# A hybrid backbone step on one core: gate prefix sums in blocks of 384 tokens, outer products two steps later

## The chip, the cores and the metric

The kernel runs on one core of one Trainium2 chip. The metric is the device time of one execution in microseconds; the lower the better. A comparison shows the median of several executions.

## What is computed

Two layers over 1152 tokens (128 context tokens and 1024 latent tokens) of width 1024. Each layer has a token mixer with three groups (attention, gated linear attention GLA, and a gated recurrence RG-LRU) that share one input projection and one output projection, and then an MLP with 4096 hidden units. The part that the change touches is GLA: for each direction, gates `g` are summed along each chunk of 64 tokens, and queries and keys are scaled by the exponentials of those sums.

```python
def gla_chunked(q, k, v, g, s0):                      # n chunks of 64 tokens, H = 4 heads of 64
    b = jnp.cumsum(g, axis=2)                         # the prefix sums, per chunk
    b_last = b[:, :, -1:]
    q_in, k_in, k_end = q * jnp.exp(b), k * jnp.exp(-b), k * jnp.exp(b_last - b)
    a_intra = jnp.where(causal, jnp.einsum('bnchd,bnshd->bnhcs', q_in, k_in), 0.0)
    o_intra = jnp.einsum('bnhcs,bnshv->bnchv', a_intra, v)
    delta = jnp.einsum('bnchd,bnchv->bnhdv', k_end, v)
    # s = exp(b_last) * s + delta, from chunk to chunk; s_before is the state ahead of a chunk
    o_inter = jnp.einsum('bnchd,bnhdv->bnchv', q_in, s_before)
    return o_intra + o_inter, s_final
# token_mixer: h @ w_in -> q k v gq gk gv gz gr lx lg; attention, gla_mixer (both directions),
# rglru_mixer (conv, two gates, scan in both directions); concat @ w_out
```

## The kernel before, and what sets its order

Activations lie with features on the partitions and tokens along the columns, in blocks of 384 tokens (`TB`; `NTB` is 3). Each projection of 128 output features is a `dense` of 24 matmuls for each block (eight slices of 128 input features, and for each the three products L156, L157, L158 of values split into a high and a low part). Its result stands in one of two PSUM banks `pd` and is evicted by VectorE (DVE) or ScalarE (ACT): gq by L491 on DVE, gr by L516 on ACT and L517 on DVE, lg by L524 to L530, k and q by L552, L553 on DVE. With two banks, the matmuls of a block can start when the block two before it is evicted.

Only TensorE's (PE's) order is written by hand; a scheduler at build time orders the other engines. The projections run in the order gv0, gk0, gz, gq0, gr0, gv1, gk1, gq1, lx0, gr1, lx1, lg0, lg1, k, v, q0 to q3. Between their matmuls everything else of the mixer is handed out in steps: `dense` calls `tick` after each half of a block (12 matmuls), and `tick` takes the next step of the first generator in a chain, up to its next `yield`. A projection has six such steps. The chain holds `gla_pair(0)` from gz on, then `gla_pair(1)`, then `lru_all` (the recurrence, for `t` = 0 and 1). A generator starts when the one ahead of it has ended. Ahead of q2 the chain is drained: whatever is left is issued at once.

`gla_pair(pair)` treats two heads (`hf` = 0, 1), both directions on the two halves of the partitions. Its steps: gate products (L592) and their logarithms (L600); `cum(hf)`, the subtract L605 (DVE for `hf` 0, GpSimd (POOL) for `hf` 1) and the prefix sums L606 (forward) and L607 (backward) as scans of all 1152 columns, with `smask` zero at the start of every chunk; six passes, one for each head and block, of `pre` (L647 and L650 on DVE, an exponential L649 on ACT), `trans` (L656 on PE, L658 on ACT) and `delta` (L667 on PE, L676, L678, L683 on ACT, L684 on POOL); `states` (scans L692); then, for each block, `intra` (L731 on PE; L733 and L737 on DVE, the sum of both directions' masked scores), `outer` (L745, L751), `headsum` (L762) and `gate` (L774). `lru_all` has the convolution L827, gate matmuls, products L868, L871, and for each direction the square root L884, a product L886 and the scan L890; then L898, L900 and the store of the result to `mixd`. The first output projection (L1218 to L1220, ahead of attention) reads `mixd` back (L1189), casts it (L1194) and splits it (L1195).

Of the kernel before, what the change touches and what calls it, by code (L numbers as in the profile page):

```python
# [10 lines left out]
ALU = mybir.AluOpType  # L11
# [10 lines left out]
NTB = T // TB  # L22
# [17 lines left out]
def blk(t, tb):  # L40
    return t[:, tb * TB:(tb + 1) * TB]
# [8 lines left out]
class Net:  # L50
# [390 lines left out]
    def mixer(self, l):  # L441
        nc, I, O, C = self.nc, self.I, self.O, self.C
# [130 lines left out]
        def gla_pair(pair, hook):  # L573
# [10 lines left out]
            mns = []  # L584
# [16 lines left out]

            def cum(hf):
                Bt = G2[:, hf]
                eng = nc.gpsimd if hf else nc.vector
                eng.tensor_tensor(Bt, Bt, mns[hf], ALU.subtract)  # L605
                nc.vector.tensor_tensor_scan(Bt[0:64], smask[0:64], Bt[0:64], 0.0, ALU.mult, ALU.add)  # L606
                nc.vector.tensor_tensor_scan(Bt[64:128, ::-1], smask[64:128], Bt[64:128, ::-1], 0.0, ALU.mult, ALU.add)  # L607
                qd, kd = B(), B()
                for d in range(2):
                    nc.sync.dma_start(kd[64 * d:64 * d + 64], self.gkd[pair][64 * hf:64 * hf + 64])  # L610
                H.append((Bt, qd, kd))

            def load_qd(hf):
                for d in range(2):
                    nc.sync.dma_start(H[hf][1][64 * d:64 * d + 64], self.gqd[pair][64 * hf:64 * hf + 64])

            cum(0)
            for _ in range(3):
                yield
            steps = [(hf, tb) for hf in range(2) for tb in range(NTB)]  # L620
            st = {}

# [19 lines left out]
            def pre(hf, tb):  # L642
                if tb == 0:
                    start(hf)
                Bt, qd, kd = H[hf]
                e = self.tn()
                nc.vector.tensor_tensor(e.rearrange("p (c s) -> p c s", s=64), blk(Bt, tb).rearrange("p (c s) -> p c s", s=64),  # L647
                                        st[hf][4][:, 6 * tb:6 * tb + 6].unsqueeze(2).to_broadcast([128, 6, 64]), ALU.subtract)
                nc.scalar.activation(e, e, AF.Exp, scale=1.0 / 16)  # L649
                nc.vector.tensor_tensor(e, blk(kd, tb), e, ALU.mult)  # L650
                return e
# [49 lines left out]
                nc.gpsimd.tensor_copy(Sc[f, 0:2], dlv[f, 0:2])  # L701

            e = pre(*steps[0])
            for _ in range(3):
                yield
            cum(1)
            prev = None
            for n in range(len(steps) + 1):
                cur = None
# [72 lines left out]
            for hf in range(2):  # L782
                As[hf] = intra(0, hf)
                yield
            yield
            for tb in range(NTB):
                oT, sq = outer(tb, As)
# [120 lines left out]
        def lru_fin():  # L908
# [5 lines left out]

        self.lru_fin = lru_fin
        order = [("gv0", ev_nat(self.gvd[0]), None), ("gk0", ev_st(self.gkd[0]), None), ("gz", ev_gz, lambda: self.add(gla_pair(0, lambda: None))),
                 ("gq0", ev_st(self.gqd[0], 0.125, "v"), None), ("gr0", ev_r(self.grd[0]), None),
                 ("gv1", ev_nat(self.gvd[1]), None), ("gk1", ev_st(self.gkd[1]), lambda: self.add(gla_pair(1, lambda: next(lin[0], None)))),
                 ("gq1", ev_st(self.gqd[1], 0.125, "v"), None), ("lx0", ev_st(self.lxd[0]), None),
                 ("gr1", ev_r(self.grd[1]), None), ("lx1", ev_st(self.lxd[1]), lambda: self.add(lru_all())),  # L920
# [19 lines left out]
        smask = gp.tile([128, T], mybir.dt.bfloat16, name="smask")  # L940
# [600 lines left out]
```

## Time and profile before

| | |
|---|---|
| median of 3 runs | 2908.7 us (2908.16 to 2912.33) |
| the profiled execution | 2908.05 us, its span 2906.2 us |
| busy share of the span | PE 95%, DVE 50%, ACT 39%, POOL 28% |
| mean granted PE clock | 0.977 of full |
| the two mixers | about 98 to 433 us and 1515 to 1856 us of the span |

PE works nearly all the time, so what counts is when it does not: the times at which it waits, and for whom, and the stretches in which its granted clock is 0.5. The DVE, ACT and POOL rows matter only where PE waits for them. A matmul of 384 columns is shown with 0.34 us but the next starts 0.17 to 0.18 us after it, since they overlap.

### The profile page before, as it was taken

Reading aid. Unit: us, or ns where it says so; the run is one execution under the profiler, and the core shown is the slowest. Engines: PE = TensorE matmul, PEld = TensorE weight load, DVE = VectorE, ACT = ScalarE, POOL = GpSimd, SP = SyncE. Lnnn points to the kernel's source line nnn. Section 1 sums busy time; section 2 is a strip of 40 time slices with the busy share of each in tenths; the row PEclk is TensorE's granted clock in tenths of the full one; section 3 lists DMA queues with packets and bytes.
Section 4 is the critical chain, followed back from the end, with each engine's and each line's share of the span. In section 5 each row is a group of like instructions: output and inputs, shape, how many; then the busy total and the mean of one; then the engine's idle time right before and its main releaser. Section 6 shows DMA issues by size and latency. Waiting matters only on the chain. (4 is left out here: it accounts for less than half of the span.)

```text
span 2906.2 us, 41527 instructions
## 1 busy us (share of the span) xinstructions
PE 2748.9 (95%) x16067; PEld 2625.6 (90%) x16067; DVE 1455.2 (50%) x2577; ACT 1119.6 (39%) x2046; POOL 802.5 (28%) x848
## 2 busy tenths in 40 slices
PE   5898899999999999999988989899899999999998
PEld 4887897889999999999987879878899999999998
DVE  7645677795332333233475547778832333233235
ACT  4645447763112212211356436477612112211223
POOL 4234447742001001100223244576311001100112
PEclk7999999999999999999999999999999999999999
DMA  7545358421321111111343643662211111111113
GB/s 263 137 124 158 99 157 253 128 80 51 95 88 38 43 44 44 44 37 44 111 120 86 175 127 102 217 210 69 73 37 44 44 44 39 42 44 44 44 37 131
DMA packets 279301, 273.64 MB, mean 94 GB/s; under 512 B 30032, under 2 KB 259008, under 8 KB 279104
## 3 DMA queue, kind: packets, MB, share of 16 engines
q1 hardware_dynamic: 278888, 270.92, 30.5%
q8 instruction: 127, 2.08, 0.3%
q14 instruction: 70, 0.57, 0.1%
q10 hardware_dynamic: 216, 0.06, 0.0%
HBM read 227.02 MB, written 43.91 MB: 93 GB/s over the span
## 5 line engine op out<-in xcount | busy, mean ns | idle before, releaser
L119 ACT CAST wh<-wr 128x1024 fp32r<-128x1024 f32 x228 | 239.0, 1048 | 923.5 <-PE pg L157 822.4
L157 PE MATMUL pg<-hl,wh 128*128 128x384 f32 x1584 | 538.3, 340 | 3.2 <-DVE hl L358 1.7
L156 PE MATMUL pg<-hh,wh 128*128 128x384 f32 x1584 | 538.4, 340 | 1.8 <-ACT hh L351 1.8
L158 PE MATMUL pg<-hh,wl 128*128 128x384 f32 x1584 | 537.3, 339 | 0.0
L1261 POOL TENSOR_TENSOR te<-te 128x384 f32<-128x384 f32 x192 | 165.9, 864 | 1332.9 <-ACT uh L1260 1332.7
L158 PE MATMUL pg<-uh,wl 128*128 128x384 f32 x1536 | 513.5, 334 | 1.7 <-DVE wl L120 1.7
L156 PE MATMUL pg<-uh,wh 128*128 128x384 f32 x1536 | 514.4, 335 | 0.6 <-ACT wh L119 0.6
L157 PE MATMUL pg<-ul,wh 128*128 128x384 f32 x1536 | 513.2, 334 | 0.0
L1283 DVE SCALAR_TENSOR_TENSOR x<-pg,mod,x 128x384 f32<-128x384 f32 (+2 forms) x512 | 254.2, 515 | 395.7 <-PE pg L158 395.4
L120 DVE TENSOR_TENSOR wl<-wr,wh 128x1024 fp32r<-128x1024 f32 x196 | 245.1, 1251 | 213.0 <-ACT wh L119 213.0
L1262 DVE TENSOR_TENSOR ul<-te,uh 128x384 fp32r<-128x384 f32 x192 | 107.1, 558 | 453.4 <-POOL te L1261 453.4
L156 PE MATMUL pd<-hh,wh 128*128 128x384 f32 x816 | 295.3, 362 | 22.2 <-DVE te L491 11.1
L157 PEld LDWEIGHTS pg<-hl,wh 128*128 128x128 f32 x1584 | 299.1, 189 | 5.6 <-DVE hl L358 3.0
L156 PEld LDWEIGHTS pg<-hh,wh 128*128 128x128 f32 x1584 | 299.3, 189 | 5.4 <-issue 3.4
L158 PEld LDWEIGHTS pg<-hh,wl 128*128 128x128 f32 x1584 | 299.3, 189 | 0.0
L156 PEld LDWEIGHTS pg<-uh,wh 128*128 128x128 f32 x1536 | 288.3, 188 | 4.3 <-DVE x L1283 1.7
L158 PEld LDWEIGHTS pg<-uh,wl 128*128 128x128 f32 x1536 | 288.3, 188 | 2.3 <-DVE wl L120 2.2
L157 PEld LDWEIGHTS pg<-ul,wh 128*128 128x128 f32 x1536 | 288.4, 188 | 0.0
L157 PE MATMUL pd<-hl,wh 128*128 128x384 f32 x816 | 285.1, 349 | 3.4 <-DVE hl L392 3.4
L158 PE MATMUL pd<-hh,wl 128*128 128x384 f32 x816 | 284.0, 348 | 0.0
L1259 ACT ACTIVATE te<-pg 128x384 f32<-128x384 f32 x192 | 93.8, 489 | 360.2 <-PE pg L158 360.2
L156 PEld LDWEIGHTS pd<-hh,wh 128*128 128x128 f32 x816 | 161.3, 198 | 30.7 <-DVE te L491 12.1
(279 smaller groups left out, 4341.7 us busy)
## 6 DMA issues: line engine op xcount, KB each, us to landing
wr<-in_w_mlp_dram SPq DMA_DIRECT2D x144, 512.0 KB, 4.0
wm<-in_w_mod_dram SPq DMA_DIRECT2D x96, 512.0 KB, 4.9
wr<-in_w_out_dram SPq DMA_DIRECT2D x48, 512.0 KB, 4.9
wr<-in_w_in_dram SPq DMA_DIRECT2D x36, 512.0 KB, 5.2
xd<-x SPq DMA_DIRECT2D x48, 192.0 KB, 3.6
x<-xd SPq DMA_DIRECT2D x48, 192.0 KB, 3.9
raw<-mixd SPq DMA_DIRECT2D x40, 192.0 KB, 2.9
B<-gkd SPq DMA_DIRECT2D x16, 288.0 KB, 4.6
```

What stands on the lines that cost most here:

```text
L119: nc.scalar.copy(hi[:, :m], raw[:, :m])
L120: lo_eng.tensor_tensor(lo[:, :m], raw[:, :m], f32(hi[:, :m]), ALU.subtract)
L156: mm(out, wh[i], xs[i][0], start=i == 0, stop=False)
L157: mm(out, wh[i], xs[i][1], start=False, stop=False)
L158: mm(out, wl[i], xs[i][0], start=False, stop=i == n - 1)
L1259: nc.scalar.activation(r, p[:, :TB], AF.Relu)
L1261: nc.gpsimd.tensor_tensor(r, r, r, ALU.mult)
L1262: nc.vector.tensor_tensor(blk(ul, tb), r, f32(blk(uh, tb)), ALU.subtract)
L1283: nc.vector.scalar_tensor_tensor(xa, p[:, a:b], self.M[l]["g2"][:, dt, s:s + 1], xa, ALU.mult, ALU.add)
```

## The change

The subtract and both scans of `cum` now run on one block of 384 columns at a time, with a `yield` after each block. Chunks of 64 tokens do not cross blocks, so that no sum is carried over. `cum(0)` takes the three steps that were empty until now. `cum(1)` was issued whole ahead of the first `trans`; now its three blocks go into the three steps behind the first `pre`. Two empty steps more stand ahead of the first `outer`, so that `gla_pair` has two steps more than before (31 instead of 29 by its yields), and `lru_all` starts four steps later.

```diff
             def cum(hf):
                 Bt = G2[:, hf]
-                eng = nc.gpsimd if hf else nc.vector
-                eng.tensor_tensor(Bt, Bt, mns[hf], ALU.subtract)
-                nc.vector.tensor_tensor_scan(Bt[0:64], smask[0:64], Bt[0:64], 0.0, ALU.mult, ALU.add)
-                nc.vector.tensor_tensor_scan(Bt[64:128, ::-1], smask[64:128], Bt[64:128, ::-1], 0.0, ALU.mult, ALU.add)
                 qd, kd = B(), B()
                 for d in range(2):
                     nc.sync.dma_start(kd[64 * d:64 * d + 64], self.gkd[pair][64 * hf:64 * hf + 64])
                 H.append((Bt, qd, kd))
+                for tb in range(NTB):
+                    b = blk(Bt, tb)
+                    eng = nc.gpsimd if hf else nc.vector
+                    eng.tensor_tensor(b, b, blk(mns[hf], tb), ALU.subtract)
+                    f, r = b[0:64], b[64:128, ::-1]
+                    nc.vector.tensor_tensor_scan(f, blk(smask, tb)[0:64], f, 0.0, ALU.mult, ALU.add)
+                    nc.vector.tensor_tensor_scan(r, blk(smask, tb)[64:128], r, 0.0, ALU.mult, ALU.add)
+                    yield
...
-            cum(0)
-            for _ in range(3):
-                yield
+            yield from cum(0)
...
             e = pre(*steps[0])
+            c1 = cum(1)
             for _ in range(3):
+                next(c1, None)
                 yield
-            cum(1)
...
             for hf in range(2):
                 As[hf] = intra(0, hf)
                 yield
+            yield
+            yield
             yield
```

The line numbers of the changed kernel are two to five higher: L611 is the subtract, L613 and L614 are the scans, L649 and L652 stand for L647 and L650, L736 and L740 for L733 and L737, L767 and L771 for L764 and L768, L891, L895, L903 and L905 for L886, L890, L898 and L900.

DVE in pair 0 of the first layer, from the eviction of gq0's first block (`te<-pd`) on; `G` holds the gates, `B` the subtrahends and `tn` the scaled keys. Before:

```order
L491 TENSOR_SCALAR te<-pd 128x384
L605 TENSOR_TENSOR G_1014<-G_1014,B 128x1152
L596 TENSOR_SCALAR B<-pg,vt_268 128x384 x3
L606 SCALAR_TENSOR_TENSOR G_1014<-smask,G_1014 64x1152
L607 SCALAR_TENSOR_TENSOR G_1014<-smask,G_1014 64x1152
L491 TENSOR_SCALAR te<-pd 128x384
L606 SCALAR_TENSOR_TENSOR G_1014<-smask,G_1014 64x1152
L647 TENSOR_TENSOR tn<-G_1014,bl 128x384
L491 TENSOR_SCALAR te<-pd 128x384
```

The same place in the changed kernel:

```order
L611 TENSOR_TENSOR G_1014<-G_1014,B 128x384 x2
L596 TENSOR_SCALAR B<-pg,vt_268 128x384 x2
L613 SCALAR_TENSOR_TENSOR G_1014<-smask,G_1014 64x384
L596 TENSOR_SCALAR B<-pg,vt_268 128x384
L614 SCALAR_TENSOR_TENSOR G_1014<-smask,G_1014 64x384
L613 SCALAR_TENSOR_TENSOR G_1014<-smask,G_1014 64x384
L614 SCALAR_TENSOR_TENSOR G_1014<-smask,G_1014 64x384
L491 TENSOR_SCALAR te<-pd 128x384
L611 TENSOR_TENSOR G_1014<-G_1014,B 128x384
L613 SCALAR_TENSOR_TENSOR G_1014<-smask,G_1014 64x384 x2
L614 SCALAR_TENSOR_TENSOR G_1014<-smask,G_1014 64x384 x2
L491 TENSOR_SCALAR te<-pd 128x384
```

Four short scans stand ahead of the second eviction instead of two long ones; the third is behind four more and a subtract, and the first L649 (was L647) behind all three evictions.

DVE in pair 1 of the first layer, between the first and the second sum of scores (L737, now L740), which the outer products read; L827 is the convolution, L524 and L530 belong to the eviction of lg. Before:

```order
L733 TENSOR_TENSOR tn<-pg,gmask 128x384
L827 SCALAR_TENSOR_TENSOR B<-B,vt_268 128x127
L827 SCALAR_TENSOR_TENSOR B<-B,vt_268 128x1023
L524 COPY te<-pd 128x384
L764 TENSOR_SCALAR ms_2603<-pg 128x6
L827 SCALAR_TENSOR_TENSOR B<-B,vt_268 128x127
L768 COPY tn<-rs_2605 128x384
L827 SCALAR_TENSOR_TENSOR B<-B,vt_268 128x1023
L530 SCALAR_TENSOR_TENSOR te<-te 128x384
L733 TENSOR_TENSOR tg<-pg,gmask 128x384
L733 TENSOR_TENSOR tn<-pg,gmask 128x384
L737 TENSOR_TENSOR tg<-tg,tn 128x384
```

The same sum in the changed kernel:

```order
L736 TENSOR_TENSOR tn<-pg,gmask 128x384
L524 COPY te<-pd 128x384
L120 TENSOR_TENSOR wl<-wr,wh 128x1024
L264 COPY mrow<-pe 128x256
L767 TENSOR_SCALAR ms_2702<-pg 128x6
L530 SCALAR_TENSOR_TENSOR te<-te 128x384
L771 COPY tn<-rs_2704 128x384
L273 TENSOR_TENSOR mod_1_2744<-pe,vt_268 128x16 x2
L736 TENSOR_TENSOR tg<-pg,gmask 128x384
L736 TENSOR_TENSOR tn<-pg,gmask 128x384
L740 TENSOR_TENSOR tg<-tg,tn 128x384
```

The convolution rows L827 have gone from this place (to L832, ahead of it), and a weight split L120 and two small copies have come in.

DVE at the end of the recurrence's second half in the first layer; L552 and L553 evict blocks of the q projections. Before:

```order
L886 TENSOR_TENSOR B<-B 128x1152
L552 STREAM_SHUFFLE te<-pd 128x384
L890 SCALAR_TENSOR_TENSOR B<-B 128x128
L890 SCALAR_TENSOR_TENSOR B<-B,vt_268 128x1024
L894 COPY lfin<-B 128x1
L553 TENSOR_TENSOR te<-pd,rope 128x384
L120 TENSOR_TENSOR wl<-wr,wh 128x1024
L898 TENSOR_TENSOR B<-B 128x1152
L548 COPY te<-pd 128x128
L900 SCALAR_TENSOR_TENSOR B<-B 128x1152
```

In the changed kernel:

```order
L891 TENSOR_TENSOR B<-B 128x1152
L895 SCALAR_TENSOR_TENSOR B<-B 128x128
L895 SCALAR_TENSOR_TENSOR B<-B,vt_268 128x1024
L899 COPY lfin<-B 128x1
L903 TENSOR_TENSOR B<-B 128x1152
L552 STREAM_SHUFFLE te<-pd 128x384
L905 SCALAR_TENSOR_TENSOR B<-B 128x1152
L553 TENSOR_TENSOR te<-pd,rope 128x384
```

The evictions of q have moved behind the scan, and the weight split L120 behind the last product. On PE, 192 projection matmuls stand between the last gate matmul of the recurrence and the first L1218 before, and 144 in the changed kernel.

## Rows read from the trace of the kernel before

**Rows 1.** Page, part 1: busy us (share of the span) and instructions of an engine.

```profile
PE 2748.9 (95%) x16067; PEld 2625.6 (90%) x16067; DVE 1455.2 (50%) x2577; ACT 1119.6 (39%) x2046; POOL 802.5 (28%) x848
```

**Rows 2.** Waits of PE: waiting line <- releasing line: us in total, times, longest us.

```profile
PE pg L667 <- ACT tg L658: 13.7, 8, 4.8
PE pg L656 <- DVE tn L650: 12.2, 4, 4.5
PE pd L156 <- DVE te L491: 11.1, 3, 5.3
PE pe L503 <- DVE lfin L894: 9.9, 2, 4.9
PE pg L745 <- DVE tg L737: 8.0, 2, 4.0
PE pd L156 <- DVE te L553: 6.2, 2, 3.1
PE pd L1218 <- DVE te L553: 5.1, 2, 2.9
```

**Rows 3.** Timeline of PE, pair 0, layer 0: start us, us, engine, line, instruction [idle before].

```profile
114.55 0.34 PE L157 MATMUL pd<-hl,wh 128*128 128x384 f32 x1
114.72 0.34 PE L158 MATMUL pd<-hh,wl 128*128 128x384 f32 x1
120.39 0.69 PE L156 MATMUL pd<-hh,wh 128*128 128x384 f32 x1 [5.32 <-DVE te L491]
...
129.32 0.49 PE L656 MATMUL pg<-ident,tn 128*128 128x128 f32 x3
...
154.94 0.83 PE L667 MATMUL pg<-vz,tg 128*128 128x128 f32 x6
```

**Rows 4.** Timeline of DVE over the same stretch.

```profile
107.97 1.36 DVE L605 TENSOR_TENSOR G<-G,B 128x1152 f32<-128x1152 f32 x1 [1.29 <-ACT G L600]
...
114.73 5.01 DVE L607 TENSOR_TENSOR_SCAN G<-smask,G 64x1152 f32<-64x1152 bf16 x1
119.77 0.56 DVE L491 TENSOR_SCALAR te<-pd 128x384 f32<-128x384 f32 x1
...
129.63 1.02 DVE L650 TENSOR_TENSOR tn<-B,tn 128x384 f32<-128x384 f32 x2
```

**Rows 5.** Timeline of POOL over the same stretch: the subtract of the second head.

```profile
114.71 2.61 POOL L605 TENSOR_TENSOR G<-G,B 128x1152 f32<-128x1152 f32 x1 [30.37 <-DVE G L606]
```

**Rows 6.** Lines L606 and L692: duration ns min/median/max, first and last start, form.

```profile
L606 DVE TENSOR_TENSOR_SCAN G<-smask,G x8: 2540/2550/2757, 112.2 to 1646.9; 64x1152 f32<-64x1152 bf16 x8
...
L692 DVE TENSOR_TENSOR_SCAN dl<-tn,dl x32: 758/767/1544, 143.9 to 1687.4; 128x304 f32<-128x304 f32 x32
```

**Rows 7.** Windows: length, busy us PE, PEld, DVE, ACT, POOL, PE clock, DMA, GB/s.

```profile
119.20:125.90 6.70, 5.51 (x17) 5.52 (x18) 6.61 (x8) 2.56 (x8) 2.80 (x2) 0.50 0.34 102
128.80:155.80 27.00, 21.08 (x132) 20.40 (x132) 13.49 (x17) 23.49 (x46) 17.00 (x18) 0.94 0.40 99
```

**Rows 8.** Timeline of PE, pair 1, layer 0: the second and third outer products.

```profile
288.04 0.52 PE L774 MATMUL pg<-ident,tn 128*128 128x128 f32 x3 [1.34 <-DVE tn L768]
...
292.90 0.47 PE L745 MATMUL pg<-tg,B 128*64 128x128 f32 x1 [3.99 <-DVE tg L737]
...
310.13 0.44 PE L745 MATMUL pg<-tg,B 128*64 128x128 f32 x4
```

**Rows 9.** Timeline of DVE there: the sum that the third outer product reads.

```profile
308.42 0.56 DVE L737 TENSOR_TENSOR tg<-tg,tn 128x384 f32<-128x384 f32 x1
```

**Rows 10.** Timeline of PE, layer 0: the last gate matmul of the recurrence.

```profile
384.88 0.34 PE L158 MATMUL pg<-tg,B 128*128 128x384 f32 x1
```

**Rows 11.** Timeline of DVE behind it: a scan and the last product.

```profile
391.69 2.32 DVE L890 TENSOR_TENSOR_SCAN B<-B,vt 128x1024 f32<-128x1024 f32 x1
...
405.94 1.34 DVE L900 SCALAR_TENSOR_TENSOR B<-B 128x1152 f32<-128x1152 f32 x1
```

**Rows 12.** Timeline of ACT: the last casts for the first output projection.

```profile
420.01 1.16 ACT L1194 CAST mh<-raw 128x384 fp32r<-128x384 f32 x2 [4.28 <-DMA raw<-mixd]
```

## Prediction

> **What bounds the kernel now.** I read the page first: TensorE (PE) is busy for 2748.9 of 2906.2 us [rows 1], so only the 157 us in which it stands, and the stretches in which it runs at the lower clock, can be won. Next I read PE's own waits [rows 2]. Those that the change can touch are the rows on L667, L656, L491, L503, L737 and the two on L553. They lie in one stage, the mixer of each of the two layers, and in four places of it, which are the four terms below.
>
> *Place A, the gates' prefix sums.* PE stops at 115.06 and goes on at 120.39, waiting for the eviction L491 of a gq0 block [rows 3]. That eviction stood on DVE behind a scan of 5.01 us [rows 4]; scans of this shape take 2.55 us [rows 6], and this one began 0.02 us after a GpSimd subtract of 2.61 us [rows 5], so about 2.5 us of it were waiting. [...] After that come the six transposes L656 and six products L667 of one pair of heads, which wait for ACT or DVE [rows 2]. There ACT is the busiest engine, 23.49 of 27.0 us [rows 7].
>
> *Place B, the outer products.* In pair 1 the second group L745 waits 3.99 us for the sum L737 on DVE [rows 8, 9], once in each layer [rows 2]. *Place C, the end of the first half of the recurrence (lru_all with t=0).* A transpose L503 waits 4.9 us for DVE [rows 2]. *Place D, the end of its second half.* After the last recurrence matmul, at 384.88 [rows 10], PE waits 3.1 us for the eviction L553 [rows 2], and again up to 2.9 us in the first output projection [rows 2].
>
> **The change part by part.** Durations are those of the profiled execution, 2908.05 us with a span of 2906.2; the median of the three runs is 2908.7, 0.65 us higher. I sum the differences and take them from the median.
>
> *Extra work on DVE.* Sixteen scans of 1152 columns become 48 of 384. Two shapes bound one of these: 2.55 us for 1152 columns, 0.767 for 304 [rows 6], so 2.1 ns per column and 0.935 us for 384. Three cost 2.81, so 0.26 more for each of 16 scans, 4.1 us in all. Four DVE subtracts of 1.36 us [rows 4] become twelve; two products of the same shape take 1.02 us [rows 4], so three cost 1.53 and the four sets 0.7 us more. This is 1.2 us for each of four stretches, on the engine on which PE waits; it counts inside A. [...]
>
> *A.* The DVE order of the changed kernel puts four scans ahead of the second L491, not two whole ones. From the subtracts' start at 107.97 [rows 4]: two subtracts 1.0, two evictions 1.1, then scans of 0.935 with the third eviction between them (it waits for ACT until about 111.6), the fourth scan ends near 115.0, and L491 (0.56 [rows 4]) frees its bank at 115.5. PE, there at 115.06, stands 0.5 us instead of 5.3 and keeps its clock. But the next L491 has a subtract and four scans ahead of it (4.2 us) and up to 2.6 us of GpSimd's subtracts, so PE waits again, 0.5 to 3 us; then two further scans stand ahead of the first product L650. I get the first transposes at about 125.7 instead of 129.32 [rows 3], a lead of 3.6 us. The second product still needs all 12 scans: 127.4 to 130.6 by the sum of DVE work, against 130.1 now [rows 4]. From there ACT has as much to do as before, and the last product L667, at 154.94 now [rows 3], comes only about 2 us earlier. With the better clock I take **2.5 us per stretch**; bounds -1 (lead lost, added scans paid) and +6 (ACT's 3.5 idle us of rows 7 go, and the 2.5 us behind GpSimd). Four stretches: +10 us.
>
> The wait of 2.5 us behind GpSimd need not come back, since three short subtracts are as long together as one. [...]
>
> *B.* The two empty steps move each pair's outer products, and pair 1 starts two steps later, so pair 1's are four steps later (two units of 24 matmuls, 8.4 us). In the new DVE order the long convolution rows (L827) stand before the first intra product, and before the second sum stands what stood before the third until now: an eviction, a weight split, L530. That third sum ended at 308.98 [rows 9] and its L745 began at 310.13 without a wait [rows 8]. The convolution rows make DVE some 2 us later than that, against 1.15 us of slack, so I expect a wait of 1 to 2 us. Gone: 3.99, and the 1.34 ahead of the transposes [rows 8], and the low clock after such a wait, 2.8 us priced as in A. **+6.5 us per layer**, bounds -2 (L530 late, and it holds DVE) and +8.4. The empty steps issue nothing; the projection's matmuls fill them.
>
> *C.* The recurrence is four steps later too. The end of its first half moves from the v to the q0 projection. L503 then has one long scan fewer ahead of it: about 2.5 us of wait instead of 4.9. But q0's first bank is evicted behind a product and a scan (2.32 us [rows 11]) of the recurrence's other direction. With the copies around them that is some 5 us after the bank is full, and I count 2.8 us of new wait there. **0 per layer**, -3.5 to +4.9.
>
> *D.* The covering work shrinks: PE's order has 192 projection matmuls between the last recurrence matmul and the first output projection now, and 144 after, 25 us at full clock. The tail behind that matmul now runs from 384.88 over the recurrence's last gate product on DVE (ends 407.28 [rows 11]) to the casts of its read-back (end 421.17 [rows 12]): 36 us. With the waits inside (3.1 as now, about 1.4 more at the third q2 block) PE reaches the output projection some 30 us after the last recurrence matmul, and the last operands come at 34 to 36. DVE has two things fewer in the tail, so I count 1.3 us of wait for operands and 2.5 for the eviction: 8.3 instead of 5.3 us. **-3 us per layer**, -9 (a full-length tail, low clock after it) to +3. SP's queue reads mixd in the same order, behind fewer stores of q.
>
> Sum: 4 x 2.5 + 2 x (6.5 + 0 - 3) = 17 us, so 2908.7 - 17 = about **2892 us**.
>
> **The rivals.** *The hand-out gives nothing.* The order runs four and five scans on end, so DVE still gates the first products and ACT the rest. A is then 0; with B at +3 and D at -3 nothing is left: 2908.7 us. For it: ACT's 23.49 of 27.0 us, and that most of the scans' sum stays ahead of the second product. Against it: PE's longest single wait, on L491, plainly shrinks.
>
> *The recurrence tail comes uncovered (slower).* Everything that lay beside 48 more projection matmuls now ends at the output projection, whose operands come through DVE, a store, a read-back, ACT and DVE again. If the tail keeps 36 us and its scans also hold q2's evictions, D is -10, C -3.5; with A + B at +8 per layer this gives 5.5 us more per layer, 2920 us. It decides from the point at which C + D exceed the 11.5 us per layer that A + B are to bring. For it: waits already stand there [rows 2], so there is little slack. Against it: in the kernel now the casts end about 4 us before PE, by the count of its 192 matmuls with that wait and its low clock, comes to them.
>
> *All waits of the gate stretches go.* If ACT's idle time was the scans' fault throughout, A is +6 or more per stretch and B +8.4: 24 + 17 - 6 = 35 us, 2874 us. ACT's load speaks against it.
>
> **How the numbers follow.** Chances: the forecast 0.52 (its own range 2880 to 2902), nothing 0.20, uncovered tail 0.20, all waits 0.08. A measurement of this kernel tells about 0.2%, 5.8 us, from no change, so faster is below 2902.9 and slower above 2914.5. Faster: 0.52 + 0.08 + 0.04 of the nothing case, 0.64. Same: 0.15 of it and 0.03 of the tail case, 0.18. Slower: 0.18. The range 2876 to 2919 leaves out about 0.08 at either end.
>
> **What would show it.** In the changed profile: PE's wait on L491 under 1 us at first, then a second one of 0.5 to 3 us; scans of 384 columns at 0.93 us; the first transposes near 125 to 126 us and the last L667 near 153; no wait over 2 us on pair 1's outer products; L503's wait about half, and a new one on a q0 eviction; the first output projection with more waiting than now, on the cast or split of its operands. I am wrong if the last L667 of a pair is not earlier (A was ACT's), if PE waits on mh or ml for over 5 us (D), or if the outer products still wait 4 us (B).

## The result and the profile after

The changed kernel takes 2928.8 us in the median of 6 runs (2925.1 to 2930.6), the kernel before 2910.0 (2908.2 to 2913.0): a ratio of 1.0063, with an interval of 1.0053 to 1.0073. It became 19 us slower. I had forecast 2892 and a range of 2876 to 2919.

More lines have other numbers in the changed kernel: L658, L660, L669 are L656, L658, L667 of before; L748, L777 are L745, L774; L853, L855 are L848, L850; L1057 is L1052; L1199, L1200, L1223 are L1194, L1195, L1218. The same line of the page as [rows 1], after:

```profile
PE 2761.1 (94%) x16067; PEld 2630.7 (90%) x16067; DVE 1464.4 (50%) x2617; ACT 1125.8 (38%) x2050; POOL 798.0 (27%) x856
```

DVE does 9.2 us more work in all (1455.2 before). That is not where 19 us go: PE stands longer, and it runs longer at the low clock (its mean granted clock is 0.974 where it was 0.977, and its busy time grew by 12 us with the same 16067 matmuls). PE's waits, the same view as [rows 2] (waiting line <- releasing line: us in total, times, longest):

```profile
PE pg L669 <- ACT tg L660: 21.9, 9, 4.7
...
PE pd L156 <- DVE te L553: 11.0, 6, 2.7
PE pg L658 <- DVE tn L652: 8.1, 5, 2.5
PE pd L156 <- DVE te L517: 7.3, 3, 3.0
...
PE pg L1085 <- DVE qs L1057: 6.8, 6, 1.3
PE pd L156 <- DVE te L491: 6.8, 4, 3.4
...
PE pg L156 <- ACT tg L853: 5.5, 2, 2.7
...
PE pe L503 <- DVE te L505: 4.9, 2, 2.5
...
PE pg L157 <- DVE tg L855: 4.4, 2, 2.2
```

Against [rows 2]: the wait on L737 (8.0 us) is gone, L491 went from 11.1 to 6.8, L503 from 9.9 to 4.9, L650 from 12.2 to 8.1. In their place stand ACT's copy L660 (13.7 before, now 21.9) and three waits that the kernel before did not have or hardly had: L517, the first operand of the recurrence's second half (L853, L855), and the queries of attention (L1057; 1.4 us before). Part of the growth at L660 is a change of name: the same products also waited 4.3 us for a DMA and 2.3 us for ACT's L683 before, and 1.5 us for the DMA now, so that all their waits together grew from 20.3 to 23.4 us.

A list of waits does not show the clock. So I also went through PE's timeline matmul by matmul: the time from its start to the next start, less the median of the same pair of lines at full clock with no wait. What is left is the time lost to standing and low clock together, and it can be summed by place. Both layers, us, worked out from the profiled executions:

```
place                                  before   after
A  gate stretches of both pairs          65.0    71.0
   outer products, pair 0                 8.1     8.4
B  outer products, pair 1                23.9    12.6
C  recurrence, first half and its end    14.7    12.4
C  recurrence, second half                0.4    16.2
D  from there to the out projection      13.2    10.6
D  first 32 products of L1218 / L1223    17.9    34.8
   rest of attention and projection      38.3    34.2
   all other parts of the program        90.5    95.9
```

Without the last row the difference is 18.7 us. The medians differ by 18.8, and these two profiled executions by 22.5. (The parts that the change does not touch differ by up to 5 us from one profiled execution to another in the runs below.) The outer products won 11 us, where 13 were forecast. All the other places together lost 30.

### The profile page after: what moved, and what is told of

Its sections match the earlier page's. It is cut to its first block, busy times and chain, and to the rows that moved or that the text cites. A ratio compares the mean times of both kernels' runs of the same rounds, so it can differ in the third digit from the quotient of the medians.

```text
span 2928.7 us, 41579 instructions
## 1 busy us (share of the span) xinstructions
PE 2761.1 (94%) x16067; PEld 2630.7 (90%) x16067; DVE 1464.4 (50%) x2617; ACT 1125.8 (38%) x2050; POOL 798.0 (27%) x856
## 5 line engine op out<-in xcount | busy, mean ns | idle before, releaser
L120 DVE TENSOR_TENSOR wl<-wr,wh 128x1024 fp32r<-128x1024 f32 x196 | 246.4, 1257 | 197.2 <-ACT wh L119 191.6
```

The lines of the kernel that those rows point to most:

```text
L120: lo_eng.tensor_tensor(lo[:, :m], raw[:, :m], f32(hi[:, :m]), ALU.subtract)
```

## The experiments

### Which part of the change, and which place

Four kernels take the change apart. `blocks_only` is the change without its two empty steps. The other three start from the kernel before:

```diff
 # steps_only: only the two empty steps of the change, in both pairs
+            yield
+            yield
             yield
             for tb in range(NTB):
                 oT, sq = outer(tb, As)
 # rec_later: four empty steps at the start of lru_all
-            yield
+            for _ in range(5):
+                yield
             nxt = lin[1]
 # half1_later: four empty steps between the recurrence's halves
                 if t:
+                    for _ in range(4):
+                        yield
                     for _ in nxt:
                         pass
```

> The change without its two empty steps: prefix sums per block and handed out, TensorE's order as before. Theory 'places': the losses of TensorE counted place by place in the two traces (standing plus low clock) say that the gate stretches got 6 us worse over both layers, so the kernel before plus 6, about 2916 us (2910 to 2920). Rival 'scans': the whole loss of 19 us comes from the smaller scans and their hand-out, 2929. The recorded forecast for this part alone: 2899.

> The kernel before with only the two empty steps ahead of the outer products. Theory 'places': outer products 11 us better, end of the recurrence's first half 13 us worse, its second half and the start of attention 11 us worse: plus 13, about 2923 us. Rival 'scans': the empty steps bring the forecast 7 us or nothing, 2902 to 2910.

> The kernel before with four empty steps ahead of the recurrence and nothing else: outer products and prefix sums stand as before, only the recurrence comes 48 projection matmuls later. Theory 'places': the two late places without the gain of the outer products, plus 24, about 2934 us. Rival 'scans': nothing, 2910. The recorded forecast for these two terms: plus 6, 2915.

> The kernel before with four empty steps between the halves of the recurrence: the first half stands as before, the second and the read-back of its result come 48 matmuls later. Theory 'places': only the last place pays, plus 11, about 2921 us, and the wait for the second half's first operand (5 us in the changed kernel) isn't there. Rival: the first half's lateness is what costs, also at the end: 2910 or a little faster.

Measured: blocks_only 2912.9 us, ratio 1.0002 (0.9992 to 1.0012); steps_only 2927.8, 1.0057 (1.0041 to 1.0073); rec_later 2936.2, 1.0082 (1.0067 to 1.0098); half1_later 2924.4, 1.0043 (1.0031 to 1.0056). The lost time by place:

```
place                        before  blocks_only  steps_only  rec_later  half1_later
A  gate stretches              65.0         66.4        70.1       68.3         67.7
B  outer products, pair 1      23.9         24.4        14.8       24.4         23.5
C  first half and its end      14.7         16.2        15.2       12.4         15.0
C  second half                  0.4          0.5        13.8       15.7          0.3
D  to the out projection       13.2         13.2        11.3       12.2         10.6
D  first 32 of out projection  17.9         18.4        34.3       35.6         38.4
   rest of attention           38.3         37.8        33.9       34.8         34.6
```

The prefix sums per block, handed out, are worth nothing either way; I had expected 6 us of loss from them. The whole loss, within the intervals, comes with two lines, the empty steps. Each place follows its own cause: the outer products gain only where the empty steps stand ahead of them; the second half's first operand is late where the recurrence as a whole is late, and not where only its second half is; the start of the out projection loses 16 to 21 us more in every kernel in which that half has 144 projection matmuls behind it instead of 192. steps_only came out 5 us above the expectation. The gate stretches may be where (+5.1), but that row is not sharp: rec_later and half1_later leave the gate stretches as they were and still stand 3.3 and 2.7 above the kernel before. A single wait tells more. PE's wait for L517 beside pair 1, an eviction of gr1, is 3.0 us in each layer of the changed kernel and 2.6 in each layer of steps_only; it is absent in the kernel before, blocks_only, rec_later and half1_later. So the empty steps of pair 0, which move pair 1's stretch by 24 projection matmuls, cost something there too, which I had put down to the scans.

### Place C: why the second half's operand is late

In the changed kernel, layer 0, timelines of PE, ACT and DVE (start us, us, engine, line, instruction, idle before):

```profile
377.49 0.45 PE L156 MATMUL pg<-tg,B 128*128 128x384 f32 x1 [2.75 <-ACT tg L853]
380.16 0.69 PE L157 MATMUL pg<-tg,B 128*128 128x384 f32 x1 [2.22 <-DVE tg L855]
```

```profile
376.93 1.34 ACT L853 CAST tg<-B 128x384 fp32r<-128x384 f32 x3 [3.38 <-DVE B L832]
```

```profile
370.52 0.54 DVE L553 TENSOR_TENSOR te<-pd,rope 128x384 f32<-128x384 f32 x1
370.98 2.02 DVE L905 SCALAR_TENSOR_TENSOR B<-B 128x1152 f32<-128x1152 f32 x1
372.92 2.30 DVE L832 SCALAR_TENSOR_TENSOR B<-B,vt 128x127 f32<-128x127 f32 x2
375.15 0.01 DVE L552 LOAD_MASK_SELECT te<-pd  x1
375.15 0.57 DVE L552 STREAM_SHUFFLE te<-pd 128x384 f32<-128x384 f32 x1
375.63 1.26 DVE L832 SCALAR_TENSOR_TENSOR B<-B,vt 128x1023 f32<-128x1023 f32 x1
376.81 0.55 DVE L553 TENSOR_TENSOR te<-pd,rope 128x384 f32<-128x384 f32 x1
377.28 1.56 DVE L120 TENSOR_TENSOR wl<-wr,wh 128x1024 fp32r<-128x1024 f32 x1
378.76 1.81 DVE L855 TENSOR_TENSOR tg<-B,tg 128x384 fp32r<-128x384 f32 x2
```

Read it upwards from PE. It waits for the cast L853 and the split L855 of the second half's input. The cast waits for the last row of that half's convolution, L832, which ends at 376.9. That row stands on DVE behind the first half's last product L905 and between the rotary evictions L552 and L553 of q0, and the split stands behind the weight split L120. DVE is never idle between 354 and 380 us. In the kernel before, the first half ended beside v, whose blocks ACT takes out of their banks, and the last row ended at 364.4, in time. Two kernels take away one thing each from the changed one:

```diff
 # taps_early: the second half's convolution two steps per block, not one
-                        if d == 0:
-                            next(nxt, None)
+                        next(nxt, None)
 # q0_act: q0's blocks copied by ACT, not rotated
-                     (f"q{i}", ev_rope(self.qd[i], False), None) for i in range(4)]
+                     (f"q{i}", ev_rope(self.qd[i], False) if i else ev_plain(self.qd[i]), None) for i in range(4)]
```

> The changed kernel, with the convolution of the recurrence's second half issued two steps per block instead of one, so all of it before the first half's final scans. Theory 'late rows': in the changed kernel the last convolution rows stand on DVE behind those scans and behind the rotary evictions of q0, and TensorE's wait of 5.0 us for the second half's first operand, with the low clock after it (2.7 us), comes from that: about 8 us per layer go, 2929 becomes 2914 (2910 to 2919). Rival 'crowding': DVE has no time left there whatever the order, the wait moves to L503 or to the evictions, 2925 to 2932.

> The changed kernel with the rotation of q0 left out: its blocks are copied out of their banks by ACT, as the v blocks are, and no longer rotated through DVE and GpSimd. Theory 'evictions': the first half's end now lies on q0, whose evictions use DVE, instead of v, whose evictions use ACT; without them the convolution rows come in time: 6 to 8 us per layer less, 2929 becomes 2914 (2910 to 2918). Rival: the scheduler has simply dealt the rows late, 2925 or more.

taps_early 2919.7 us, 1.0030 (1.0020 to 1.0040), just above its range; q0_act 2911.0, 1.0000 (0.9991 to 1.0009). In both the second half loses nothing to speak of (0.3 and 1.1 us instead of 16.2). In taps_early 4.3 us of it come back at the first half's end, where L503 waits again:

```profile
PE pe L503 <- DVE te L505: 5.5, 1, 5.5
```

(The profiled execution of taps_early, 2915.0 us, is the fastest of its nine, so that its places show more than the 9 us by which its median lies under the changed kernel's.) In q0_act that row is 2.5 us and nothing else stands there over 0.6, and the place loses 8.6 us instead of 12.4. So both theories hold: the rows were late because of what stood ahead of them, and the evictions were what filled DVE. With q0's rotation gone the changed kernel is as fast as the kernel before, though place D is as bad as ever (36.1 us).

### Place D: the start of the out projection

The changed kernel, layer 0: windows from the first L1223 on, in two pieces (length, busy us of PE, PEld, DVE, ACT, POOL, clock, DMA share, GB/s):

```profile
429.60:448.20 18.60, 14.30 (x66) 12.66 (x65) 14.29 (x31) 8.58 (x14) 3.23 (x4) 0.82 0.88 266
448.20:478.20 30.00, 24.11 (x118) 18.96 (x118) 22.62 (x60) 22.98 (x55) 19.77 (x26) 0.89 0.72 226
```

The kernel before, the same products:

```profile
425.10:439.70 14.60, 12.40 (x65) 12.08 (x64) 12.38 (x29) 8.85 (x18) 5.29 (x9) 0.88 0.88 278
439.70:465.10 25.40, 21.25 (x120) 17.67 (x119) 21.53 (x58) 20.28 (x46) 18.20 (x20) 0.93 0.83 250
```

That is 48.6 us against 40.0. PE's waits in it after, from 425 to 470 us:

```profile
PE pg L1085 <- DVE qs L1057: 3.3, 3, 1.3
PE pg L1117 <- DVE pl L1112: 2.1, 3, 1.3
PE pd L1223 <- ACT mh L1199: 1.4, 1, 1.4
PE pd L1223 <- DVE te L553: 1.3, 1, 1.3
PE pg L1108 <- POOL P L1099: 1.2, 1, 1.2
PE pd L1224 <- DVE ml L1200: 0.5, 1, 0.5
```

No single wait is long. Together they are 9.8 us; in the kernel before, the waits of the same products are 6.3. The low clock adds about 3 us more: by the windows' mean clocks, 6.7 us of the clock were not granted after (0.18 of 18.6 and 0.11 of 30.0) and 3.5 before. The operands of the out projection, mh and ml, cost 1.9 us, and attention behind it waits seven more times. On DVE:

```profile
428.89 0.56 DVE L1200 TENSOR_TENSOR ml<-raw,mh 128x384 fp32r<-128x384 f32 x1 [2.12 <-ACT mh L1199]
...
433.74 0.56 DVE L1200 TENSOR_TENSOR ml<-raw,mh 128x384 fp32r<-128x384 f32 x1 [0.49 <-ACT mh L1199]
434.33 1.72 DVE L1057 TENSOR_TENSOR qs<-te,qs 64x384 fp32r<-64x384 f32 x3
...
437.40 2.09 DVE L1011 TENSOR_TENSOR kl<-kraw,kh 128x1536 fp32r<-128x1536 f32 x1
```

In the kernel before, the first four splits L1195 ended at 421.8, and the keys' split L1006 began at 425.06, both before or as the out projection started. Now the last of the four ends at 434.3 and the keys follow at 437.4, 8 us behind the start. As the two timelines read, the recurrence's tail pushed the splits, these pushed attention's first work, and PE arrives there on time. No run takes one link of this chain out; what the runs vary is the cover, the number of projection matmuls behind the last recurrence matmul. A smaller dose of it:

```diff
 # half1_2: as half1_later, with two empty steps
-                    for _ in range(4):
+                    for _ in range(2):
                         yield
```

> The kernel before with two empty steps between the halves of the recurrence instead of the four of the run half1_later (168 projection matmuls of cover behind the last recurrence matmul; 192 before, 144 with four). If the cover decides by a threshold (in the kernel before the last splits of the read-back end 3.3 us before TensorE wants them, two steps are 8.4 us less at full clock for four, 4.2 for two), then nearly nothing is lost: 2910 to 2914. If each step costs alike, half of the 13 to 14 us: 2917.

2918.8 us, 1.0035 (1.0022 to 1.0048), above both expectations, though the interval reaches down to the second. Two steps cost about 9 us by the medians (10 by the ratio), four 14 (12.5 by the ratio). So nothing is free up to two steps, as a threshold would have it, and the 3.3 us between the splits' end and the out projection in the kernel before were no measure of what the place can spare. The waits of half1_2 are on evictions and on attention, none on mh or ml (first 32 products 27.9 us, from 17.9).

### Place A: why the earlier scans bring nothing

PE in pair 0 of layer 0 after, and two windows around it:

```profile
114.01 0.44 PE L156 MATMUL pd<-hh,wh 128*128 128x384 f32 x1 [0.76 <-DVE te L491]
...
120.37 0.45 PE L156 MATMUL pd<-hh,wh 128*128 128x384 f32 x1 [1.86 <-DVE te L491]
...
124.76 0.55 PE L658 MATMUL pg<-ident,tn 128*128 128x128 f32 x3 [2.00 <-DVE tn L652]
...
153.77 1.65 PE L669 MATMUL pg<-vz,tg 128*128 128x128 f32 x6 [4.73 <-ACT tg L660]
```

```profile
104.60:124.70 20.10, 15.53 (x86) 14.57 (x84) 17.84 (x23) 12.42 (x21) 4.95 (x5) 1.00 0.50 133
124.70:155.20 30.50, 22.22 (x127) 20.36 (x127) 14.52 (x21) 24.39 (x49) 15.45 (x18) 0.91 0.35 89
```

The front of the stretch went as forecast: 0.76 and 1.86 us of waiting on L491 instead of 5.32 [rows 3], the clock at 1.00. This stretch begins 1.8 us earlier after (104.6 against 106.4). The first transposes come 4.6 us earlier than in [rows 3], 2.8 by the stretch's own start; the last product 1.2 earlier, 0.6 later by its own start. The lead is spent between them. The wait of 4.73 us at the last product is not new in size; in the kernel before it stood one step earlier, at the last transposes:

```profile
150.52 0.87 PE L656 MATMUL pg<-ident,tn 128*128 128x128 f32 x3 [4.46 <-DVE tn L650]
```

Three kernels, all from the one before, each leave out one load of the stretch:

```diff
 # no_scan: no prefix scans for the second head
-                nc.vector.tensor_tensor_scan(Bt[0:64], smask[0:64], Bt[0:64], 0.0, ALU.mult, ALU.add)
-                nc.vector.tensor_tensor_scan(Bt[64:128, ::-1], smask[64:128], Bt[64:128, ::-1], 0.0, ALU.mult, ALU.add)
+                if not hf:
+                    nc.vector.tensor_tensor_scan(Bt[0:64], smask[0:64], Bt[0:64], 0.0, ALU.mult, ALU.add)
+                    nc.vector.tensor_tensor_scan(Bt[64:128, ::-1], smask[64:128], Bt[64:128, ::-1], 0.0, ALU.mult, ALU.add)
 # one_exp: one exponential for both products
-                for sg, dst, src in ((-1, qd, qd), (1, st[hf][3], kd)):
-                    e = self.tn()
-                    nc.scalar.activation(e, blk(Bt, tb), AF.Exp, scale=sg / 16)
+                e = self.tn()
+                nc.scalar.activation(e, blk(Bt, tb), AF.Exp, scale=-1 / 16)
+                for sg, dst, src in ((-1, qd, qd), (1, st[hf][3], kd)):
 # short_turn: one of the four scans over a head's states
-                for q in range(4):
+                for q in range(1):
                     v = dl[:, n * q:n * q + n]
```

> The kernel before with the two prefix scans of the second head of each pair left out (8 scans of 2.55 us gone from DVE). The recorded forecast took it that the scans hold the gate stretches: by it at least 5 us per stretch go, 20 us in all, 2890. Theory 'ACT and its chain': the stretch's end is set by ACT and by ACT and GpSimd handing the exponents to each other, and the scans' end only moves the waits: at most 2 us per stretch, 2902 to 2911.

> The kernel before with one exponential per block of a gate stretch instead of two (both products use the same one, so the results are not the reference's): 6 of 0.51 us less on ACT in each stretch, 3 us. Theory 'ACT sets the end of the stretch': 2 to 4 us per stretch with the low clock, 8 to 16 in all, 2895 to 2903. Rival: the turn from one head to the next (states' scan, copies, the next head's copies into the same tile) sets it whatever ACT has to do, at most 1 us per stretch: 2906 to 2911.

> The kernel before with three of the four scans over the states of each head left out (2.7 us of DVE less at each turn from one head to the next; results not the reference's). Theory 'turn': the gate stretch ends when the chain products, states' scan, copies of the states, next head's copies into the same tile has run, so its shortening shows: 2 to 4 us per stretch, 8 to 16 in all, 2895 to 2902. Rival 'no single owner': scans, exponentials and the turn each hold a part, and what one gives is taken by the next: at most 1.5 us per stretch, 2904 to 2911.

no_scan 2908.1 us, 0.9990 (0.9981 to 0.9999); one_exp 2904.7, 0.9981 (0.9972 to 0.9991); short_turn 2887.1, 0.9926 (0.9909 to 0.9943). Lost time by place:

```
place                        before  no_scan  one_exp  short_turn
A  gate stretches              65.0     61.2     62.9        57.9
B  outer products, pair 1      23.9     24.2     22.0        10.8
```

With half of the scans gone altogether, 5 us of DVE per stretch, a stretch loses 1 us less (0.6 by the median). DVE is then idle in it and waits for GpSimd, and the last product of the pair waits as in the changed kernel, about as long as the transposes did before (timelines of DVE and PE in no_scan, line numbers one higher than before's):

```profile
131.69 0.56 DVE L648 TENSOR_TENSOR tn<-G,bl 128x384 f32<-128x384 f32 x1 [4.23 <-POOL B L685]
...
137.23 0.56 DVE L648 TENSOR_TENSOR tn<-G,bl 128x384 f32<-128x384 f32 x1 [0.96 <-POOL B L685]
```

```profile
152.76 1.65 PE L668 MATMUL pg<-vz,tg 128*128 128x128 f32 x6 [4.57 <-ACT tg L659]
```

Removing 3 us of ACT brings 0.5 us per stretch, removing 2.7 us of DVE at the turn between the heads 1.8. one_exp fell between the two expectations: 1.3 us per stretch by the median, 0.5 by place. No one load that was left out owns the stretch; the largest share measured is the turn's. (In the kernels of this document whose gate stretches are as before, this row stands at 66.5 to 68.6 us, against 65.0, so that only short_turn's 57.9 and no_scan's 61.2 are clear of the scatter.)

short_turn is faster than its theory by 8 us because place B is relieved as well: the wait of 3.99 us of [rows 8] is 0.84 there. The time of the state scans left out does not explain this by itself, since in the kernel before DVE stands idle twice between the second head's scans and the sum L737, which ends only at 292.85:

```profile
262.58 2.84 DVE L692 TENSOR_TENSOR_SCAN dl<-tn,dl 128x304 f32<-128x304 f32 x4 [6.04 <-ACT dl L678]
...
272.76 1.23 DVE L120 TENSOR_TENSOR wl<-wr,wh 128x1024 fp32r<-128x1024 f32 x1 [3.96 <-ACT wh L119]
...
279.19 0.69 DVE L812 TENSOR_TENSOR B<-B 128x512 fp32r<-128x512 f32 x1 [5.20 <-ACT B L811]
```

What differs is DVE's order behind that: in short_turn all six convolution rows L827 stand ahead of the four products L733 of that sum, where in the kernel before four of them stand among these. The scheduler dealt them so, as in the changed kernel; what this order is worth alone is not shown, and only place A tells of the turn.

### The gain without the loss

If the places are independent, the empty steps should be kept in pair 1 and two steps taken out behind its last block, so that the recurrence does not move:

```diff
 # outer_only, from the kernel before (outer_blocks: the same in the changed one)
             yield
+            for _ in range(2 if pair else 0):
+                yield
             for tb in range(NTB):
@@ the pair's closing step
-            yield
+            if not pair:
+                yield
@@ lru_all
                 pass
-            yield
             nxt = lin[1]
```

> The kernel before with the two empty steps in pair 1 alone, and two steps taken out behind its last block (the pair's closing one and the first of the recurrence), so that the recurrence's matmuls stand where they stood. Theory 'places': the gain of the outer products without the losses of the recurrence: 4 to 5 us per layer, about 2901 us, and the out projection starts with 9 us lost per layer as before. Rival: the gain exists only because the recurrence no longer holds DVE there, 2910.

> The changed kernel with its two empty steps in pair 1 alone and two steps taken out behind its last block, so that the recurrence stands where it stood before; prefix sums per block and handed out as in the change. Theory 'places': the prefix sums are worth nothing, the outer products their 4 to 5 us per layer, the recurrence loses nothing: 2901 us (2898 to 2905). If the changed prefix sums cost something once the rest is healthy, 2905 to 2912.

> The run outer_only with the recurrence's second half two steps earlier (two of the first half's closing steps merged) and its convolution issued two steps per block, so that it is done by then: 216 projection matmuls of cover instead of 192. Theory 'cover': the start of the out projection and of attention, where 9 us per layer are still lost, gets 1 to 4 us per layer better, and the second half's first matmul doesn't wait: 2892 to 2898 against 2900. Rival: DVE is crowded at the first half's end, and the wait on L503 grows by what is won: 2900 to 2906.

outer_only 2900.3 us, 0.9966 (0.9956 to 0.9977); outer_blocks 2903.1, 0.9977 (0.9968 to 0.9986); best1 2906.5, 0.9984 (0.9975 to 0.9994). Lost time by place, us, with the two kernels that come last:

```
place                        before  outer_only  outer_blocks  best1  v_act  taps_v
A  gate stretches              65.0        67.4          66.9   68.6   66.6    66.5
   outer products, pair 0       8.1         4.1           5.5    4.7    3.9     3.4
B  outer products, pair 1      23.9         9.6          10.2   11.1    9.1     9.9
C  first half and its end      14.7        17.2          17.2    9.5   16.4     8.8
C  second half                  0.4         0.4           0.5   11.3    1.1     0.4
D  to the out projection       13.2        13.2          13.1   10.5   13.1    15.8
D  first 32 of out projection  17.9        18.3          18.1   22.4   19.3    17.4
```

(The row of pair 0's outer products falls only because the normal times are taken from each kernel by itself; with one set of normal times for all kernels it is 7.9 us before and 7.5 to 9.5 in these five, and B's gains are about 1 us smaller.) outer_only is where it was expected, and better than both kernels; with the change's prefix sums it is the same within the intervals. best1 missed both expectations: with 216 matmuls of cover the way to the out projection and its first products lose 32.9 us, against 31.5 in outer_only, and the second half, asked for earlier, waits for its operand again (2.4 us and the low clock, in each layer). PE also waits for evictions where its closing steps were merged (2.6 us for L498 in each layer). In this kernel more cover than 192 brings nothing; in the kernels above less costs.

The wait on L503 at the first half's end (5.3 us in outer_only) was tried last, from outer_only: v_act puts the copy behind it, L505, on ACT for v, and taps_v adds the edit of taps_early.

```diff
 # v_act
-                    nc.vector.tensor_copy(t2, p2[:, :TB])
+                    (nc.scalar.copy if cache is not None else nc.vector.tensor_copy)(t2, p2[:, :TB])
```

> The run outer_only with the last copy of the v blocks (the one behind the transposes) on ACT instead of DVE. Theory 'DVE is the queue at the first half's end': TensorE's wait of about 5 us on the transposes of v there is only this copy standing behind the recurrence's scans, and ACT is idle for 8 us at that time, so the wait and its low clock go: 6 us per layer, 2900 becomes 2888 (2885 to 2893). Rival: TensorE arrives earlier at the rotary evictions of q0 and waits there instead: 2894 to 2901.

> The run v_act with the second half's convolution issued two steps per block, as in taps_early. In v_act ACT stood 9.8 us at a cast that waits for the last convolution row on DVE, which stands there behind the recurrence's scans, with the copies of the v blocks queued behind the cast. Theory 'queue': with the convolution done early neither ACT nor DVE holds a v copy, the wait of 5.6 us goes in both layers, with its low clock: 2901 becomes 2889 (2886 to 2895). Rival: TensorE comes earlier to the rotary evictions of q0 on DVE and waits there: 2896 to 2902.

v_act 2901.4 us, 0.9975 (0.9966 to 0.9984): nothing gained. PE's wait is no longer on L503 but on ACT's copy L498 of the next v block, for 5.6 us, and ACT shows why:

```profile
357.02 0.51 ACT L850 CAST tg<-B 128x384 fp32r<-128x384 f32 x1 [9.82 <-DVE B L830]
357.44 1.04 ACT L119 CAST wh<-wr 128x1024 fp32r<-128x1024 f32 x1
358.38 0.47 ACT L498 COPY te<-pd 128x384 f32<-128x384 f32 x1
```

ACT stood 9.8 us at a cast that waits for the convolution on DVE, and the copy was queued behind that cast. taps_v 2895.5 us, 0.9951 (0.9935 to 0.9968): with the convolution earlier ACT stands there 4.4 us and PE 2.6, the place loses 8.8 us instead of 16.4, and 2.7 come back on the way to the out projection, so that it ends between the expectation's range and the rival's. It is the fastest kernel of the study that computes the whole reference, 13 us under the kernel before and 33 under the changed one.

## Why the prediction was wrong, point by point

Between the forecast of 2892 us and the measured 2929 lie 37 us. By place, A holds 16 of them, C 13.5, D 4 and B 2.

**A, +10 us expected, -6 measured.** The scans were read rightly: 0.95 us for 384 columns (0.935 in the sum), L491's two waits 0.76 and 1.86 (0.5, and 0.5 to 3), first transposes 2.8 us earlier (3.6). The step that failed is the next one, from that lead to 2.5 us per stretch. I had written that ACT has as much to do as before and that the last product comes 2 us earlier; I credited the clock on top. no_scan shows that even taking half of the scans away brings 1 us per stretch, and the wait of 4.5 to 4.7 us at the pair's last transposes or products stays in all three kernels. The sign that I had named, a last L667 that is not earlier, came true by the stretch's own start (0.6 us later). The loss of 6 is not of the scans (blocks_only 1.4 us by place, none by the median), and it is all in pair 1: counted by pair, pair 0 loses about 1.5 us less than before and pair 1 about 6.5 more. There the empty steps of pair 0 move the stretch against the evictions of gr1, and a wait of 3.0 us on L517 appears in each layer. How much of the 6 us is the row's scatter (up to 3.6) stays open. The prediction moved pair 1's outer products by these steps, and not its gates.

**GpSimd.** The scan beside its subtract took 5.01 us where such scans take 2.55 [rows 4, 6]. These 2.5 us did not all go, and the premise that three short subtracts are as long as one, which was my assumption, did not hold in this stretch: they took 4.16 us together where one took 2.61 [rows 5], and two scans beside them 3.39 where two take 1.9. So 1.5 us remained on DVE and GpSimd paid as much more. What made these scans longer is not shown by any run.

**B, +13 expected, +11 measured.** Right in place and nearly in size: no group of outer products waits any more (the second L748 starts at 302.94, right behind the transposes L777), where I had still counted 1 to 2 us, and outer_only shows the gain by itself. The 2.8 us in the sum for the low clock behind the wait are shown by no run at this place: before, the clock was granted at 0.50 there from 292.9 to 296.6 us, so that 1.9 us were not granted. In short_turn the wait nearly goes too (0.84 us), with the convolution rows in the order that I had counted on.

**C, 0 expected, -13.5 measured, outside its bounds of -7 to +9.8 for two layers.** Both waits that I priced came: L503's halved (2.45 us), and one on q0's eviction (1.1 us for the 2.8 expected). What I did not follow was the third user of DVE in that stretch, the convolution L827 of the second half, on which the next matmuls of the recurrence depend. With the low clock it costs 8 us per layer (in taps_early and q0_act, where it comes in time, the second half loses 0.3 and 1.1 us over both layers). Counting a queue for two of its waiters and not for the third is the step that failed.

**D, -6 expected, -10.2 measured, within its bounds.** The wait for operands (1.4 and 0.5 us for 1.3) and for the eviction (1.3 for 2.5) are about as counted, and PE comes to the out projection as late as I said. But the sum ended at its first operands. Attention's first queries and keys come behind them, and there PE waits seven more times in layer 0: the step that failed here is where the sum stops. That the missing cover is the cause is shown (half1_2 and half1_later lose more with each step of it); that the same tail pushes the queries and keys is read from the timelines and not tested link by link.

**The rival** called "the recurrence tail comes uncovered" came nearest, with 0.20: it named a place and the sign, but only part of the mechanism, since the output projection's operands cost 1.9 us per layer and most of C's loss lay at the convolution. It priced C at -3.5 and D at -10 per layer where they measured -6.8 and -5.1, and credited A and B with 8 per layer where they brought 2.6. Its 2920 us was therefore 9 too low, and the range, which I drew around these prices, ended at 2919.

## What to carry to other kernels

A step added to a serial hand-out moves everything behind it: list all its consumers, also those of the next stage, and price each engine's queue for every instruction that someone waits for, not for the two waits that the trace shows today. Delay only the work whose operands come late, and take the steps out again behind it, as in outer_only. A wait that is followed to one engine should be tested by taking that engine's load away before a saving is credited: here half of the scans was worth 1 us per stretch.

## What the runs showed that I had not expected

Moving an instruction off a busy engine can move the wait with it: in v_act ACT was idle for 9.8 us, and PE waited 5.6 us, as long as on DVE (5.3), for a copy queued on ACT behind one cast. And the low clock added to a small wait: where PE stood 5.0 us for the operand in place C, the window around it ran at a mean clock of 0.68, and the place lost 8 us per layer, 3 more than it stood:

```profile
374.70:385.40 10.70, 5.74 (x18) 5.43 (x18) 5.87 (x8) 4.97 (x8) 4.62 (x3) 0.68 0.41 142
```
